# Filler work beside attention heads: smaller weight splits asked for earlier, less of it ahead of the heads and more inside them, and waits per tile in the pools

## The chip, the cores and the metric

One core of one Trainium2 chip runs the kernel. The metric is the device time of one execution in microseconds (us). The engines are TensorE (PE, with its weight loads PEld), VectorE (DVE), ScalarE (ACT), GpSimd (POOL) and SyncE (SP), whose queue issues nearly all DMAs, in order.

## The reference

One block of a hybrid conformer, for 1024 tokens of width 1024, float32:

```
h = rms_norm(x); z = h @ w_in            # glu, q, k, v, gate logits
a = silu(rms_norm(causal_conv31(a_val * sigmoid(a_gate))))
y_a = a @ w_conv_out
o = three dilated window attentions, mixed by softmax of their lse   # 16 heads of 64
y_b = o @ w_attn_out
x = x + (g_a * y_a + g_b * y_b) @ w_out  # g = sigmoid(gate_logits + gate_b)
x = x + (silu(u_gate) * u_val) @ w_down  # u = causal_conv3(rms_norm(x) @ w_up)
```

The three windows of a head are computed as one masked attention: `mask[h]` holds, for each distance, what is added to a score.

## The kernel before

**Precision and its price.** Every product is made from two parts: `split` (L74) rounds a float32 tile to `hi` on ACT and takes `lo = src - hi` on DVE. A product is then three matmuls (hi*hi, hi*lo, lo*hi), and each weight piece of 128x1024 costs one DMA (`stage`, L79, recorded at L81, four `raw` buffers), one ACT and one DVE instruction (`wpiece`, L90). `gemm_half` (L103) makes a 128x512 result in 8 steps of three 128x512 matmuls (L108 to L110), and yields after each step, so that a caller can place steps one by one.

**Stages.** First come the norm, the transposes, the GLU and the q, k, v products, with the 31-tap convolution on DVE beside them (L366); q, k and v are spilled to DRAM. Then attention, then the merge with the output projections (L596 to L660), the up-projection (L670 to L800) and the down-projection (L806 on). Each stage has a tile pool of its own (`ph1`, `ph2` at L458, `hb2` at L596, `ph3` at L597, `ph4r`, `ph4`, `ph5`; `hb1` from the start).

**Filler.** Two products have no part in attention and are cut into steps: the gates (16 pieces of `w_ch`, two halves each, `gate_steps`, L146) and the convolution's output (8 pieces of `w_co`, in `side_work`, L459): 384 steps in all. A gate result goes to DRAM as `dgate`, a convolution output as `dya`. Some steps stand ahead of the heads: COVER = (24, 16, 52) are the steps taken before the convolution branch ends, between its two norm parts, and after the eight `da` spills (L428, L439, L454; the spills at L453). The rest is taken inside the heads by `fill`: FILL = (5.5, 9.5) sets how many steps a half head takes, 15 a head. What is left over runs behind the last head. The convolution's output needs `aT`, which `load_split` (L165) reads back from `da` and splits, 1024 columns at a time.

**Heads.** `head` (L486) loads q, kh, kl (two halves each), the mask m and v of one head by `fetch` (L132, recorded at L133), two buffers of each. `step` (L546) works on half a head: for each of four query tiles `score` (L501) makes q*kh and q*kl into PSUM (L507, L508), DVE adds the mask and reduces (L512), ACT takes the exponent in place (L514), DVE the reciprocal (L515) and POOL scales (L516). Beside it, `flip` (L519) transposes the scaled tiles of the half head before on PE (L523) and splits them (ph on ACT L76, pl on DVE L77), and `weigh` (L530) multiplies v by both (L531, L532). The output pair goes to DRAM (`do`, L578) after every second head. Between these, `fill` places filler steps:

```
rate = FILL[0] / 14 if prev is not None and prev[1] else FILL[1] / 10
```

**Merge.** `load_split` reads o back (`raw_o`), `merge` (L604) loads the two gates and y_a (`gg`, L608 to L610), multiplies o by the pieces of w_attn_out (`yb`, weights `raw_ao`, `hi_ao`, `lo_ao`) and forms the sum.

**What orders the work.** A scheduler with a model of the engines' times puts the instructions of each engine and each DMA queue into one fixed order when the kernel is built; the order of the program text is the priority. Pools decide waits: in a pool that reuses memory of an earlier pool, an instruction waits for what used that memory. Waits are attached to the instructions of the fixed orders.

Of the kernel before, what the change touches and what calls it, by code (L numbers as in the profile page):

```python
# [12 lines left out]
F32 = mybir.dt.float32  # L13
F32R = mybir.dt.float32r
AF = mybir.ActivationFunctionType
ALU = mybir.AluOpType
# [4 lines left out]
P = 128  # L21
D = 1024
T = 1024
# [8 lines left out]

LAG = 2
PEND = 2
FILL = (5.5, 9.5)
COVER = (24, 16, 52)


C_CW = 0
# [11 lines left out]
def block_kernel(ctx: ExitStack, tc: tile.TileContext, x, g1, g2, pack, mask,  # L51
# [13 lines left out]
    def bank_ps(name):  # L65
        return psB.tile([P, 512], F32, tag="B", name=name)
# [7 lines left out]
    def split(hi, lo, src):  # L74

        act.activation(hi, src, AF.Copy)  # L76
        dve.tensor_tensor(out=lo, in0=src, in1=hi.bitcast(F32), op=ALU.subtract)  # L77

    def stage(src, name):  # L79
        raw = wp.tile([P, 1024], F32, tag="raw", bufs=4, name=f"raw_{name}")  # L80
        sp.dma_start(raw.rearrange("p (a b) -> p a b", a=src.shape[1]) if len(src.shape) == 3 else raw, src)  # L81
        return raw
# [20 lines left out]
    def gemm_half(o, w, actT, half):  # L103

        hi, lo = w
        ah, al = actT[0][half], actT[1][half]
        for k in range(KT):
            pe.matmul(o, hi[:, k, :], ah[:, k, :], start=(k == 0), stop=False)  # L108
            pe.matmul(o, hi[:, k, :], al[:, k, :], start=False, stop=False)  # L109
            pe.matmul(o, lo[:, k, :], ah[:, k, :], start=False, stop=(k == KT - 1))  # L110
            yield
# [34 lines left out]
    def gate_steps(hT):  # L146
        def gate(c, w, half):
            gp = bank_ps(f"gate_{c}_{half}")
            yield from gemm_half(gp, w, hT, half)
            sg = cst.tile([P, 512], F32, tag="f2", bufs=2, name=f"gs_{c}_{half}")  # L150
            act.activation(sg, gp, AF.Identity, bias=pk[:, C_GB + c : C_GB + c + 1])
            sp.dma_start(dgate[c][:, half * 512 : half * 512 + 512], sg)

        for c in range(12):
            w = wpiece(w_ch[16 + c], f"gt{c}")
            for half in range(2):
                yield from gate(c, w, half)
        ws = [wpiece(w_ch[16 + c], f"gt{c}") for c in range(12, 16)]
        for half in range(2):
            for c in range(12, 16):  # L160
                yield from gate(c, ws[c - 12], half)
            if half == 0:
                yield "half"
# [11 lines left out]
    hb1_cm = tc.tile_pool(name="hb1", bufs=1, side="right")  # L175
    hb1 = hb1_cm.__enter__()

    def hb_tiles(pl, name):
        t = [[pl.tile([P, KT, 512], F32R, tag=f"hb{a}{h}", name=f"{name}{a}{h}") for a in range(2)]
             for h in range(2)]  # L180
        return [[t[h][a] for h in range(2)] for a in range(2)]


    with tc.tile_pool(name="ph1", bufs=1) as p1:
# [239 lines left out]
                    if t is not None:  # L424
                        qkv_tail(*t)
        assert all(t is None for t in tails)
        gates = gate_steps(hT)
        for _ in range(COVER[0]):  # L428
            next(gates)
        conv_acc = conv_branch()  # L430
# [24 lines left out]
            next(gates)  # L455


    with tc.tile_pool(name="ph2", bufs=1) as p2:  # L458
        def side_work():  # L459

            left = []
            for t in gates:
                if t == "half":
                    aT = hb_tiles(hb1, "aT")
                    left = list(range(0, KT, 2))
                    wait = 0
                elif left:
                    if wait == 0:
                        load_split(aT, da, 0, "a", [left.pop(0)])
                    wait = (wait + 1) % 7  # L470
                yield
            assert not left
            left = list(range(0, KT, 2))
            for c0 in (0, 4):
                ws = [wpiece(w_co[c], f"co{c}") for c in range(c0, c0 + 4)]
                for half in range(2):
                    for c in range(c0, c0 + 4):
                        if left:
                            load_split(aT, da, 1, "a", [left.pop(0)])
                        yp = bank_ps(f"ya_{c}_{half}")  # L480
                        yield from gemm_half(yp, ws[c - c0], aT, half)
                        ya = cst.tile([P, 512], F32, tag="f2", bufs=2, name=f"ya_{c}_{half}")
                        act.activation(ya, yp, AF.Copy)
                        sp.dma_start(dya[c][:, half * 512 : half * 512 + 512], ya)

        def head(h):  # L486
            hp, r, g8 = h // 2, (h % 2) * DH, h // 8
            q = p2.tile([P, T], F32R, tag="q", bufs=2, name=f"q_{h}")
            kh = p2.tile([P, T], F32R, tag="kh", bufs=2, name=f"kh_{h}")
            kl = p2.tile([P, T], F32R, tag="kl", bufs=2, name=f"kl_{h}")  # L490
            m = p2.tile([P, T], F32, tag="m", bufs=2, name=f"m_{h}")
            v = p2.tile([P, 8, P], F32R, tag="v", bufs=2, name=f"v_{h}")
            for s in range(2):
                fetch(q[s * DH : (s + 1) * DH, :], dq[g8][s][r : r + DH, hp % 4, :])
                fetch(kh[s * DH : (s + 1) * DH, :], dk[g8][0][r : r + DH, hp % 4, :])
                fetch(kl[s * DH : (s + 1) * DH, :], dk[g8][1][r : r + DH, hp % 4, :])
            sp.dma_start(m, mask[h])
            fetch(v, dv[h // 8][:, h % 8, :, :])
            return q, kh, kl, v, m

        def score(h, tiles, i):  # L501
            q, kh, kl, v, m = tiles
            nk = (i + 1) * P
            s = big_ps(f"s_{h}_{i}")
            for c0 in range(0, nk, 512):
                n = min(512, nk - c0)
                pe.matmul(s[:, c0 : c0 + n], q[:, i * P : (i + 1) * P], kh[:, c0 : c0 + n], start=True, stop=False)  # L507
                pe.matmul(s[:, c0 : c0 + n], q[:, i * P : (i + 1) * P], kl[:, c0 : c0 + n], start=False, stop=True)  # L508
# [3 lines left out]
            dve.tensor_tensor_reduce(out=pt, in0=s[:, :nk], in1=m[:, u0 : u0 + nk], scale=-1.0, scalar=3e38,  # L512
                                     op0=ALU.add, op1=ALU.min, accum_out=st[:, 0:1])
            act.activation(pt, pt, AF.Exp, bias=st[:, 0:1], scale=-1.0, accum_out=st[:, 1:2])  # L514
            dve.reciprocal(st[:, 2:3], st[:, 1:2])  # L515
            pool.tensor_scalar(pt, pt, st[:, 2:3], 1.0, op0=ALU.mult, op1=ALU.mult)  # L516
            return pt

        def flip(h, half, pts, kt):  # L519
            q0 = max(0, kt - half * 4)  # L520
            pp = bank_ps(f"pp_{h}_{half}_{kt}")
            for qb in range(q0, 4):
                pe.transpose(pp[:, qb * P : (qb + 1) * P], pts[qb][:, kt * P : (kt + 1) * P], ident)  # L523
# [3 lines left out]
            split(ph[:, c], pl[:, c], pp[:, c])  # L527
            return kt, ph, pl, c

        def weigh(o, v, nkt, kt, ph, pl, c):  # L530
            pe.matmul(o[:, c], v[:, kt, :], ph[:, c], start=(kt == 0), stop=False)  # L531
            pe.matmul(o[:, c], v[:, kt, :], pl[:, c], start=False, stop=(kt == nkt - 1))  # L532

        filler = side_work()

        credit = [0.0]

# [55 lines left out]
            pass  # L593


    hb2 = ctx.enter_context(tc.tile_pool(name="hb2", bufs=1))  # L596
    with tc.tile_pool(name="ph3", bufs=1) as p3:  # L597
        oT = hb_tiles(hb2, "oT")
        for half in range(2):
            load_split(oT, do_, half, "o")  # L600
# [105 lines left out]
        p4r_cm = tc.tile_pool(name="ph4r", bufs=1, side="right")  # L706
# [24 lines left out]
        transpose_raw(*tails.pop(0))  # L731
        assert not tails

    with tc.tile_pool(name="ph4", bufs=1) as p4:
# [68 lines left out]
    p4r_cm.__exit__(None, None, None)  # L803


    with tc.tile_pool(name="ph5", bufs=1) as p5_:  # L806
# [180 lines left out]
```

## Time and profile before

| | |
|---|---|
| time, median of 3 runs | 1809.56 us (1807.88 to 1813.9) |
| the profiled execution | 1811.24 us |
| its span on the core | 1809.5 us |
| mean granted PE clock | 0.992 |
| instructions | 22485 |
| PE busy, 575 to 950 us (heads) | 363.94 of 375 us |

A row of a group reads: line, engine, operation, output <- inputs, shape, count | busy us, mean ns of one | idle time of the engine just before, and what ended it. A row of a timeline: start in us, duration, engine, line, operation, and in brackets the wait ahead of it with what ended it. A row of a window: from and to, length, then busy us and (x number of instructions) of PE, PEld, DVE, ACT and POOL, the granted PE clock, the busy share of the DMA engines and GB/s. A row of waits: engine, instruction, what it waited for, total us, times, longest.

### The profile page before, as it was taken

The page shows a single profiled execution, that of the slowest core. Times are in us where ns is not written, and L with a number is a line of the kernel's source. Part 1 is how long each engine was busy: PE and PEld are TensorE (multiplying, and loading weights), DVE is VectorE, ACT ScalarE, POOL GpSimd, SP SyncE. Part 2 cuts the span into 40 slices and gives each one's busy share as a digit, 9 for nine tenths or more (in the row PEclk, how much of TensorE's full clock was granted, in tenths as well). Part 3 has the DMA queues.
Part 4 walks back from the last instruction along what each step waited for, and adds up shares of the span by engine and source line. Part 5 has one row for each costly group of instructions (what it writes and reads, how often), then busy time and mean ns, then how long its engine had stood idle before and what let it go on. Part 6 is the DMA issues. An engine that isn't in the chain of part 4 may idle for free.

```text
span 1809.5 us, 22485 instructions
## 1 busy us (share of the span) xinstructions
PE 1771.3 (98%) x8248; PEld 1464.5 (81%) x8248; DVE 1320.5 (73%) x1801; ACT 771.8 (43%) x1203; POOL 194.5 (11%) x197
## 2 busy tenths in 40 slices
PE   8999999999999999999999999989999999999999
PEld 6888888888877888878888878768888888878887
DVE  6999999999635656665645543787777777789863
ACT  5111132223245656665655332545444554543441
POOL 1000142132002212222210000210000000000000
PEclk9999999999999999999999999999999999999999
DMA  5111145345468546664527543312222122389851
GB/s 210 49 49 47 41 134 175 105 134 169 139 200 246 135 136 177 201 195 142 152 78 268 179 152 134 99 47 108 79 82 82 71 95 91 116 304 333 298 181 47
DMA packets 141920, 257.05 MB, mean 142 GB/s; under 512 B 11249, under 2 KB 60529, under 8 KB 141810
## 3 DMA queue, kind: packets, MB, share of 16 engines
q1 hardware_dynamic: 141808, 255.61, 43.6%
q8 instruction: 65, 1.06, 0.2%
q14 instruction: 45, 0.37, 0.1%
q10 hardware_dynamic: 2, 0.00, 0.0%
HBM read 189.51 MB, written 66.06 MB: 141 GB/s over the span
## 4 chain that ended last, share of the span: by engine, by line
PE 53%; DMA 4%; DVE 3%; issue 1%; ACT 1%; SPq 1%; POOLq 0%; POOL 0%; DVEq 0%; ACTq 0%
PE xz L673 5%; PE xz L674 5%; PE xz L675 5%; PE dx L832 5%; PE dy L832 5%; DMA gg<-dya 2%; PE pp L523 2%; PE y L673 2%; PE y L675 2%; PE y L674 2%; PE ya L108 2%; PE ya L109 2%; PE ya L110 2%; PE wo L126 2%; PE o L531 2%; PE wo L125 2%
## 5 line engine op out<-in xcount | busy, mean ns | idle before, releaser
L366 DVE SCALAR_TENSOR_TENSOR cacc<-apad,pk,cacc 128x1024 f32<-128x1024 f32 x240 | 298.1, 1278 | 0.7
L125 PE MATMUL qkv<-hi_qkv,hT 128*128 128x512 f32 x384 | 151.9, 397 | 0.0
L127 PE MATMUL qkv<-hi_qkv,hT 128*128 128x512 f32 x384 | 150.5, 392 | 0.0
L126 PE MATMUL qkv<-lo_qkv,hT 128*128 128x512 f32 x384 | 149.5, 390 | 0.0
L512 DVE CUSTOM_DVE_ANT_0 p<-s,m 128x128 f32<-128x128 f32 (+7 forms) x128 | 95.2, 751 | 67.3 <-PE pp L523 43.4
L77 DVE TENSOR_TENSOR pl<-pp,ph 128x512 fp32r<-128x512 f32 x192 | 102.9, 550 | 48.9 <-ACT ph L76 48.4
L76 ACT ACTIVATE ph<-pp 128x512 fp32r<-128x512 f32 x192 | 90.9, 487 | 96.4 <-PE pp L523 92.3
L516 POOL TENSOR_SCALAR p<-p,st 128x128 f32<-128x128 f32 (+7 forms) x128 | 94.8, 749 | 339.8 <-DVE st L515 219.5
L772 DVE SCALAR_TENSOR_TENSOR u<-u,pk 128x1023 f32<-128x1023 f32 (+1 forms) x88 | 112.4, 1280 | 18.8 <-ACT u L770 18.5
L101 POOL TENSOR_TENSOR rs<-ss,mhalf 128x8 f32<-128x8 f32 x32 | 73.8, 2311 | 338.0 <-DVE ss L100 338.0
L514 ACT ACTIVATE p<-p,st 128x128 f32<-128x128 f32 (+7 forms) x128 | 99.0, 775 | 15.8 <-DVE st L512 14.0
L108 PE MATMUL gate<-hT,hi_gt 128*128 128x512 f32 x256 | 102.6, 401 | 0.0
L109 PE MATMUL gate<-hT,hi_gt 128*128 128x512 f32 x256 | 101.5, 396 | 0.0
L110 PE MATMUL gate<-hT,lo_gt 128*128 128x512 f32 x256 | 100.8, 395 | 0.0
L523 PE MATMUL pp<-ident,p 128*128 128x128 f32 x576 | 94.0, 276 | 0.0
L127 PEld LDWEIGHTS qkv<-hi_qkv,hT 128*128 128x128 f32 x384 | 72.1, 188 | 15.5
L126 PEld LDWEIGHTS qkv<-lo_qkv,hT 128*128 128x128 f32 x384 | 72.2, 188 | 14.4
L125 PEld LDWEIGHTS qkv<-hi_qkv,hT 128*128 128x128 f32 x384 | 72.2, 188 | 14.0
L507 PE MATMUL s<-kh,q 128*128 128x512 f32 (+1 forms) x192 | 69.6, 367 | 9.5 <-DVE st L512 6.2
L523 PEld LDWEIGHTS pp<-ident,p 128*128 128x128 f32 x576 | 69.2, 142 | 10.0 <-issue 0.2
L531 PE MATMUL o<-ph,v 128*128 128x512 f32 x192 | 72.9, 380 | 3.8 <-ACT ph L76 1.6
L532 PE MATMUL o<-pl,v 128*128 128x512 f32 x192 | 70.4, 368 | 1.8 <-DVE pl L77 1.8
(289 smaller groups left out, 4612.8 us busy)
## 6 DMA issues: line engine op xcount, KB each, us to landing
wr<-w_down SPq DMA_DIRECT2D x45, 512.0 KB, 5.8
gr<-dff SPq DMA_DIRECT2D x62, 256.0 KB, 5.4
raw_qkv<-w_qkv SPq DMA_DIRECT2D x24, 512.0 KB, 4.1
raw_uv<-w_up SPq DMA_DIRECT2D x22, 512.0 KB, 3.2
raw_ug<-w_up SPq DMA_DIRECT2D x22, 512.0 KB, 3.2
dff<-u SPq DMA_DIRECT2D x22, 512.0 KB, 2.6
dv<-v SPq DMA_DIRECT2D x16, 512.0 KB, 3.2
raw_gt<-w_ch SPq DMA_DIRECT2D x16, 512.0 KB, 4.6
```

Source lines behind the costliest of these rows:

```text
L108: pe.matmul(o, hi[:, k, :], ah[:, k, :], start=(k == 0), stop=False)
L109: pe.matmul(o, hi[:, k, :], al[:, k, :], start=False, stop=False)
L110: pe.matmul(o, lo[:, k, :], ah[:, k, :], start=False, stop=(k == KT - 1))
L125: pe.matmul(ps, ah, hi[:, k % 2, :], start=(k == 0), stop=False)
L126: pe.matmul(ps, ah, lo[:, k % 2, :], start=False, stop=False)
L127: pe.matmul(ps, al, hi[:, k % 2, :], start=False, stop=(k == KT - 1))
L366: dve.scalar_tensor_tensor(out=acc, in0=a[:, j : j + T], scalar=w(j), in1=acc, op0=ALU.mult, op1=ALU.add)
L523: pe.transpose(pp[:, qb * P : (qb + 1) * P], pts[qb][:, kt * P : (kt + 1) * P], ident)
L673: pe.matmul(o, wh[:, k, :], bh[:, k, :], start=(start and k == 0), stop=False, skip_group_check=not start)
L674: pe.matmul(o, wh[:, k, :], bl[:, k, :], start=False, stop=False, skip_group_check=not start)
L675: pe.matmul(o, wl[:, k, :], bh[:, k, :], start=False, stop=(k == 3), skip_group_check=not start)
L832: pe.matmul(banks[n], a[:, c], b[:, d], start=(start and i == 0 and m == 0), stop=(stop and i == nf - 1 and m == 2), skip_group_check=True)
```

## The change

- **Halves.** `wpiece2` splits a filler weight in two halves of 512 columns each, and `load_split` does the same for `aT` and o.
- **Pieces ahead.** `ahead` takes a list of uses (weight, name, consumer) and asks for weight pieces up to two ahead of the one in use, at most four in hand.
- **One filler.** Gates and convolution output are joined into one generator, `side_steps`, made before the convolution ends. The loads of `aT` are spread, one with each half-1 gate of the last four pieces and then one with each convolution output.
- **How much, where.** COVER is (24, 16, 20) instead of (24, 16, 52), FILL (6.5, 11.5) instead of (5.5, 9.5): 18 steps a head.
- **Order.** The score's reduce and exponent, and the split of a flipped block, are issued with `high_priority(URGENT)`, 120.
- **Pools.** `hb1`, `ph2`, `hb2`, `ph3`, `ph4r`, `ph4` and `ph5` are made with `reuse_waits="tile"`, so that a tile waits for the earlier tiles whose memory it takes and not for the whole pool's; q, kh, kl, v and the first four p tiles go to a pool of their own, `ph2in`.

Line numbers are some 20 higher behind the new functions.

```diff
-FILL = (5.5, 9.5)
-COVER = (24, 16, 52)
+FILL = (6.5, 11.5)
+COVER = (24, 16, 20)
+URGENT = 120
...
+    HALVES = (slice(0, 512), slice(512, 1024))
+    def wpiece2(src, name):
+        raw = stage(src, name)
+        hi = wp.tile([P, 1024], F32R, tag="whi", bufs=4, name=f"hi_{name}")
+        lo = wp.tile([P, 1024], F32R, tag="wlo", bufs=4, name=f"lo_{name}")
+        for c in HALVES:
+            split(hi[:, c], lo[:, c], raw[:, c])
+        return [t.rearrange("p (a b) -> p a b", a=KT) for t in (hi, lo)]
+    def ahead(uses, more=2):
+        keys = list(dict.fromkeys(n for _, n, _ in uses))
+        src = {n: w for w, n, _ in uses}
+        last = {n: i for i, (_, n, _) in enumerate(uses)}
+        got = {}
+        for i, (_, n, consumer) in enumerate(uses):
+            while len(got) < min(len(keys), keys.index(n) + 1 + more):
+                k = len(got)
+                if k >= 4 and last[keys[k - 4]] >= i:
+                    break
+                got[keys[k]] = wpiece2(src[keys[k]], keys[k])
+            yield from consumer(got[n])
+    def side_steps(hT, da):
+        aT = []
+        left = [(h, k) for h in range(2) for k in range(0, KT, 2)]
+        def gate(c, half):
+            def go(w):
+                gp = bank_ps(f"gate_{c}_{half}")
+                if c >= 12 and half == 1:
+                    if not aT:
+                        aT.extend(hb_tiles(hb1, "aT"))
+                    load_split(aT, da, 0, "a", [left.pop(0)[1]])
+                yield from gemm_half(gp, w, hT, half)
...
+        return ahead([gate(c, half) for c in range(12) for half in range(2)]
+                     + [gate(c, half) for half in range(2) for c in range(12, 16)]
+                     + [conv_out(c, half) for c0 in (0, 4) for half in range(2) for c in range(c0, c0 + 4)])
...
             raw = stage(src[:, k : k + 2, half * 512 : half * 512 + 512], f"{name}{half}{k}")
-            split(dst[0][half][:, k : k + 2, :], dst[1][half][:, k : k + 2, :],
-                  raw.rearrange("p (a b) -> p a b", a=2))
+            for i, c in enumerate(HALVES):
+                split(dst[0][half][:, k + i, :], dst[1][half][:, k + i, :], raw[:, c])
...
-        gates = gate_steps(hT)
+        gates = side_steps(hT, da)
...
-    with tc.tile_pool(name="ph2", bufs=1) as p2:
+    with tc.tile_pool(name="ph2", bufs=1, reuse_waits="tile") as p2, \
+            tc.tile_pool(name="ph2in", bufs=1, reuse_waits="tile") as p2i:
...
-            q = p2.tile([P, T], F32R, tag="q", bufs=2, name=f"q_{h}")
+            q = p2i.tile([P, T], F32R, tag="q", bufs=2, name=f"q_{h}")
...
-            pt = p2.tile([P, nk], F32, tag=f"p{i}", bufs=1, name=f"p_{h}_{i}")
+            pt = (p2i if i < 4 else p2).tile([P, nk], F32, tag=f"p{i}", bufs=1, name=f"p_{h}_{i}")
...
+            with tc.high_priority(URGENT):
+                dve.tensor_tensor_reduce(out=pt, in0=s[:, :nk], in1=m[:, u0 : u0 + nk], scale=-1.0, scalar=3e38,
+                                         op0=ALU.add, op1=ALU.min, accum_out=st[:, 0:1])
+                act.activation(pt, pt, AF.Exp, bias=st[:, 0:1], scale=-1.0, accum_out=st[:, 1:2])
...
+            with tc.high_priority(URGENT):
+                split(ph[:, c], pl[:, c], pp[:, c])
...
-        filler = side_work()
+        filler = gates
...
-    hb2 = ctx.enter_context(tc.tile_pool(name="hb2", bufs=1))
-    with tc.tile_pool(name="ph3", bufs=1) as p3:
+    hb2 = ctx.enter_context(tc.tile_pool(name="hb2", bufs=1, reuse_waits="tile"))
+    with tc.tile_pool(name="ph3", bufs=1, reuse_waits="tile") as p3:
```

The same argument is added to `hb1`, `ph4r`, `ph4` and `ph5`.

More of the change, by code (lines that the diff above doesn't have):

```diff
@@ L144, in block_kernel @@
     dx2 = [dr.tile([P, D], F32, name=f"dx2_{i}") for i in range(8)]
[L146 to L163, printed above, removed]
+    HALVES = (slice(0, 512), slice(512, 1024))
@@ L168, in load_split @@
             raw = stage(src[:, k : k + 2, half * 512 : half * 512 + 512], f"{name}{half}{k}")
-            split(dst[0][half][:, k : k + 2, :], dst[1][half][:, k : k + 2, :],
-                  raw.rearrange("p (a b) -> p a b", a=2))
+            for i, c in enumerate(HALVES):
+                split(dst[0][half][:, k + i, :], dst[1][half][:, k + i, :], raw[:, c])
     edge = ctx.enter_context(tc.tile_pool(name="edge", bufs=1, side="right"))
     edge.tile([P, 248], F32, name="edge")
-    hb1_cm = tc.tile_pool(name="hb1", bufs=1, side="right")
+    hb1_cm = tc.tile_pool(name="hb1", bufs=1, side="right", reuse_waits="tile")
     hb1 = hb1_cm.__enter__()
@@ L455, in block_kernel @@
             next(gates)
-    with tc.tile_pool(name="ph2", bufs=1) as p2:
[L459 to L484, printed above, removed]
+    with tc.tile_pool(name="ph2", bufs=1, reuse_waits="tile") as p2, \
+            tc.tile_pool(name="ph2in", bufs=1, reuse_waits="tile") as p2i:
         def head(h):
             hp, r, g8 = h // 2, (h % 2) * DH, h // 8
-            q = p2.tile([P, T], F32R, tag="q", bufs=2, name=f"q_{h}")
-            kh = p2.tile([P, T], F32R, tag="kh", bufs=2, name=f"kh_{h}")
-            kl = p2.tile([P, T], F32R, tag="kl", bufs=2, name=f"kl_{h}")
+            q = p2i.tile([P, T], F32R, tag="q", bufs=2, name=f"q_{h}")
+            kh = p2i.tile([P, T], F32R, tag="kh", bufs=2, name=f"kh_{h}")
+            kl = p2i.tile([P, T], F32R, tag="kl", bufs=2, name=f"kl_{h}")
             m = p2.tile([P, T], F32, tag="m", bufs=2, name=f"m_{h}")
-            v = p2.tile([P, 8, P], F32R, tag="v", bufs=2, name=f"v_{h}")
+            v = p2i.tile([P, 8, P], F32R, tag="v", bufs=2, name=f"v_{h}")
             for s in range(2):
@@ L705, in block_kernel @@
         hb1_cm.__exit__(None, None, None)
-        p4r_cm = tc.tile_pool(name="ph4r", bufs=1, side="right")
+        p4r_cm = tc.tile_pool(name="ph4r", bufs=1, side="right", reuse_waits="tile")
         p4r = p4r_cm.__enter__()
@@ L732, in block_kernel @@
         assert not tails
-    with tc.tile_pool(name="ph4", bufs=1) as p4:
+    with tc.tile_pool(name="ph4", bufs=1, reuse_waits="tile") as p4:
         for n in ("b22", "t4"):
@@ L803, in block_kernel @@
     p4r_cm.__exit__(None, None, None)
-    with tc.tile_pool(name="ph5", bufs=1) as p5_:
+    with tc.tile_pool(name="ph5", bufs=1, reuse_waits="tile") as p5_:
         keep3 = {}
```

18 lines of the change are left out of this document (14 added, 4 removed).

## The prediction, made before the changed kernel was run

> **What bounds the kernel now.** I read the page's engine totals first, then the table of 50-us windows, then TensorE's waits for the stretch that the change touches.
>
> ```profile
> PE 1771.3 (98%) x8248; PEld 1464.5 (81%) x8248; DVE 1320.5 (73%) x1801; ACT 771.8 (43%) x1203; POOL 194.5 (11%) x197
> 100.00:150.00 50.00, 50.00 (x222) 41.39 (x222) 47.95 (x41) 7.13 (x7) 0.00 (x0) 1.00 0.15 50
> 500.00:550.00 50.00, 45.01 (x198) 36.37 (x197) 18.80 (x31) 22.27 (x30) 0.67 (x2) 0.96 0.67 211
> 1150.00:1200.00 50.00, 40.70 (x174) 31.33 (x173) 46.34 (x45) 26.10 (x36) 14.03 (x6) 0.93 0.22 74
> 575.00:950.00 375.00, 363.94 (x1960) 305.87 (x1959) 227.84 (x582) 229.90 (x496) 86.77 (x116) 0.99 0.53 154
> ```
>
> A window row gives its length, then busy time and instructions of PE, PEld, DVE, ACT and POOL, then the granted clock. TensorE (PE) is busy 98% of the span, and a full window holds 222 matmuls in 50 us: one 128x512 matmul every 0.225 us. The changed order issues the same matmuls, so their sum cannot move; only the holes can. PE's 38.2 idle us (1809.5 - 1771.3) lie in a few places: 5.0 in 500 to 550, where the heads begin, 11.06 in 575 to 950, the heads (375 - 363.94), 9.3 in 1150 to 1200, the rest at both ends and in single waits. A hole also costs clock: the heads run at 0.99, which is up to 3.6 us more (1% of 363.94). So the heads can give about 15 us at most, and the question is which holes close and which open.
>
> ```profile
> PE s L507 <- DVE st L512: 6.2, 9, 1.3
> PE s L507 <- DMA kl<-dk: 3.0, 1, 3.0
> PE o L532 <- DVE pl L77: 1.8, 1, 1.8
> PE o L531 <- ACT ph L76: 1.6, 2, 1.1
> PE o L531 <- DVE op L575: 1.5, 5, 0.6
> PE y L674 <- DVE blk_t L77: 4.7, 1, 4.7
> PE y L673 <- ACT hi_s L76: 2.6, 1, 2.6
> ```
>
> These are PE's waits by kind (total us, times, longest), the first five from 500 to 960. In the heads, scores wait for the reduce of VectorE (DVE) two scores back, and weighings for the split of the flipped block. The one long wait is head 0's first load.
>
> **Part 1: COVER 52 to 20, the start of attention.** Thirty-two steps of three matmuls leave the cover ahead of the heads; in the changed kernel's order of PE, 72 of those 96 matmuls stand behind the first score instead of ahead of it, 72 x 0.225 = 16.2 us. They are work that still has to be done, so the start gains or loses by one comparison: how much earlier the first score can begin against 16.2 us of work not yet done.
>
> ```profile
> 540.59 0.39 PE L110 MATMUL gate<-hT,lo_gt 128*128 128x512 f32 x1
> 543.97 0.47 PE L507 MATMUL s<-kh,q 128*128 128x128 f32 x2 [3.00 <-DMA kl<-dk]
> 545.05 0.47 PE L508 MATMUL s<-kl,q 128*128 128x128 f32 x2 [0.61 <-DMA kl<-dk]
> 526.45 1.06 SPq L152 DMA_DIRECT2D dgate<-gs  x1
> 532.79 0.51 SPq L133 DMA_DIRECT2D q<-dq  x1
> 536.44 0.60 SPq L133 DMA_DIRECT2D kl<-dk  x1
> L453 SPq DMA_DIRECT2D da<-cacc x8: 319/320/1012, 517.0 to 525.9; - x8
> DMA to landing us min/median/max: 2.6/3.3/6.8
> DMA to landing us min/median/max: 3.9/5.5/7.1
> DMA to landing us min/median/max: 6.4/7.5/8.5
> SPq L133 <- DMA da<-cacc: 5.1, 2, 3.9
> ```
>
> The three landing rows are those of da, q and kl. Today the last cover matmul is issued at 540.59, the first score at 543.97. SyncE's queue (SP) issues DMAs in order. Up to the gate spill issued at 526.45 (dgate of piece 4, first half) the two kernels' queues agree: eight da spills, a weight load, this spill. In before, the loads of head 0 then wait for da to land and for a second gate spill, so that q goes at 532.79 and the second kl at 536.44. In after the eight loads stand directly behind the 526.45 spill, each with a wait for its own tile. So they can issue from about 527.5, which the edit is right about: 5.3 us earlier.
>
> But the landing gains less. The last da spill, issued at 525.9, lands 6.8 us later at 532.7; with the gate spill behind it that is about 533.3. In before the loads land some 1.3 us apart: the second q at 535.2 + 7.1 = 542.3, the second kl two loads later at 536.44 + 8.5 = 544.9. If the six loads queue behind the spills at that pace, the fifth, the second kh, which the first score needs, lands at 533.3 + 5 x 1.25 = 539.5. The other end is loads that do not queue at all: the second kl issued at 527.5 + 3.65 = 531.2 (same spacing as 532.79 to 536.44), landing the shortest q time later, 3.9, at 535.1. The late end is no gain at all, 543.97. Cost = first score's move + 16.2: 539.5 - 543.97 + 16.2 = **+11.7** (+7.3 to +16.2). I take 11.7, since the queue was full in just these microseconds (kl's landings of 6.4 to 8.5 against q's first 3.9). PE, whose cover would end at 540.8 - 16.2 = 524.6, would stand idle about 15 us in one piece. Nothing fills that hole: PE's order is fixed, and behind the cover come only scores and flips until the first softmax is through, because the next filler's PSUM bank comes after those of the flips.
>
> [...]
>
> ```profile
> 551.17 0.41 PE L523 MATMUL pp<-ident,p 128*128 128x128 f32 x1
> 544.00:552.00 8.00, 6.32 (x19) 4.75 (x20) 4.64 (x16) 4.50 (x11) 2.08 (x4) 0.63 1.05 275
> ```
>
> From the second kl to the first flip 6.1 us pass (545.05 to 551.17), with 16 score matmuls in them; in after only the 8 of the first four scores stand there, so some 8 x 0.225 = 1.8 us more are uncovered: **+2** (0 to +5, the whole chain less the score matmuls). The granted clock is 0.63 over these 8 us, 3.0 us lost, after a hole of 3.0; it will be lost again after the longer hole, so it is no difference. [...]
>
> **Part 2: the heads (FILL, halves, URGENT, two pieces ahead).** Each head carries 18 filler steps instead of 15: 16 x 9 = 144 matmuls more, which are the 96 of the cover and 48 of the stretch behind the last head.
>
> ```profile
> L77 DVE TENSOR_TENSOR lo_gt<-raw_gt,hi_gt 128x1024 fp32r<-128x1024 f32 x16 | 20.1, 1256 | 16.5 <-ACT hi_gt L76 16.5
> L77 DVE TENSOR_TENSOR pl<-pp,ph 128x512 fp32r<-128x512 f32 x96 | 64.9, 686 | 28.3 <-ACT ph L76 27.9
> L76 ACT ACTIVATE hi_gt<-raw_gt 128x1024 fp32r<-128x1024 f32 x16 | 16.9, 1056 | 24.8 <-PE gate L109 23.5 <-PE qkv L127 1.3
> L76 ACT ACTIVATE ph<-pp 128x512 fp32r<-128x512 f32 x96 | 56.1, 595 | 53.9 <-PE pp L523 51.9 <-PE o L532 0.6
> 809.87 3.49 DVE L77 TENSOR_TENSOR aT<-raw_a,aT 128x1024 fp32r<-128x1024 f32 x3
> 800.00:850.00 50.00, 46.74 (x235) 38.80 (x236) 30.24 (x76) 30.16 (x64) 12.74 (x17) 0.93 0.63 186
> ```
>
> A weight split is 1.26 us of DVE in one piece today; in halves it would be 2 x 0.69 = 1.37 (priced by the 128x512 row), on ACT 2 x 0.60 = 1.19 against 1.06. For some 40 pieces that is 5 us on each, hidden by 147 idle us of DVE in the heads (375 - 227.84) unless it falls ahead of a reduce. The holes come from such splits: three aT splits make one block of 3.49 us, and that window loses most, 3.3 us idle at a clock of 0.93. Halving helps if something urgent comes between the halves. In the changed order it mostly doesn't: 26 of 32 filler pieces of the heads have both halves side by side on DVE, 17 of 25 such blocks stand directly ahead of a score's reduce (before: 9 of 18), and one block of three to four pieces (4.8 us by these durations) is left. What does help: 18 steps instead of 15 put about 1.4 us more PE work between a score and its flip (16.6 to 18.0 us, counted in PE's order), and 0.2 more between flip and weighing, which covers most waits of 1.3 us at most. Of the 15 us I take a third, **-6**; the ends are -15 (all holes close) and +5 (seven more blocks at 0.69 each). URGENT's edit has the same answer: it is seen only in the order, which these counts use.
>
> **Part 3: the stretch behind the last head.**
>
> ```profile
> 947.73 0.32 SPq L578 DMA_DIRECT2D do<-op  x1
> 962.04 2.00 SPq L81 DMA_DIRECT2D raw_ao<-w_ao  x2
> 974.60 0.39 PE L108 MATMUL yb<-oT,hi_ao 128*128 128x512 f32 x1
> L77 DVE TENSOR_TENSOR lo_ao<-raw_ao,hi_ao x4: 1224/1226/1226, 969.6 to 975.7; 128x1024 fp32r<-128x1024 f32 x4
> DMA to landing us min/median/max: 3.9/5.2/7.0
> ```
>
> Behind the last weighing stood 125 matmuls of conv_out up to the first yb; in after 77 are left, 48 x 0.225 = 10.8 us less. What they hide is a chain: last do spill at 947.73, reload of o, the first w_ao piece at 962.04, 5.2 us of landing, its hi, its lo from 969.6, so ready at 970.8, while yb begins at 974.60: 3.8 us to spare. If the chain keeps its length, 10.8 - 3.8 = 7.0 us open up. It can be shorter, as fewer gate and dya transfers stand ahead of w_ao in SP's queue; but a dya spill is still ahead of it, ready only about 5.4 us before yb by PE's order, and a raw buffer must be free. So 4 to 6 us of hole plus up to 2 of clock: **+6** (0 if w_ao moves up by the whole 7; +11 if the spill that is ready 5.4 us before yb heads the full 8.8 us from w_ao's issue to its lo, and the clock falls).
>
> **Part 4: waits per tile in the later pools.** The last 2687 matmuls of PE stand in the same order. The largest hole there, 9.3 us in 1150 to 1200, has DVE at 46.34 of 50 us and waits for blk_t and hi_s, which no pool releases: **0** (-4 to +1).
>
> **Sum.** 11.7 + 2 - 6 + 6 = +13.7. The profiled execution took 1811.24 (span 1809.5 and 1.74 around it), 1.68 above the median of 1809.56. On the median: 1809.56 + 13.7 = 1823.
>
> **Rivals.** A measurement of this kernel can tell about 0.3% from no change, 5.4 us: faster is under 1804.1, slower over 1815.0.
>
> *Faster.* The DVE blocks stop being ahead of anything that PE needs soon: with 1.4 us more work between score and flip, and the longest score wait 1.3 us, all holes of the heads close: -15. Loads land at the early end (+7.3), the last chain shrinks by 7 (0): 1809.56 - 7.7 = 1802. For it: waits that short are easily covered. Against it: it needs three ends at once, and the da spills are in the queue. It decides when start and last stretch together cost under 9.6 us: 1 in 10.
>
> *The same.* The start costs 11.7 and 2, the first w_ao load moves up fully (0), and the heads give 12: +1.7, 1811. For it: SP's queue is less loaded behind the last head. 0.14.
>
> *Slower still.* The doubled number of split blocks directly ahead of a reduce decides in the heads (+5), with 11.7 + 2 at the start and 8 behind the heads: +26.7, 1836. For it: 17 such blocks against 9, one of 4.8 us. Against it: URGENT moves reduces ahead of what is not yet begun, and DVE has 39% idle. 0.07.
>
> *That the change doesn't do what it says*: halves side by side are whole splits, so the halving alone gives nothing; it is in the forecast already, as the -6 comes from the steps.
>
> **How the numbers follow.** The forecast has 0.69 and its own range 1815 to 1832; of it 0.02 fall within 0.3%, if the first loads come early. So faster 0.10, same 0.14 + 0.02 = 0.16, slower 0.67 + 0.07 = 0.74. The range leaves out the faster case and the end of the worst: 1806 to 1834, which takes in the unknown ends of landing (7.3 to 16.2) and of the last chain (0 to 11).
>
> **What would show it.** The wait of the first score for kl should be near 15 us, with PE's last gate matmul ahead of it near 525 and the first score at 539 to 540; a first score near 535 is the early end. The heads' idle time should go from 11 us to 5 to 8, with fewer waits for st. The first yb should wait for lo_ao or hi_ao for 4 to 6 us, and the window 1150 to 1200 should keep its 9.3 idle us, shifted. It would be wrong if PE had other work in the first hole, if the waits for st grew, or if the yb wait were absent.

## The result and the profile after

The changed kernel takes 1823.81 us (median of 4 runs, 1821.63 to 1824.43), the kernel before 1809.0 in the same comparison: ratio 1.0076, interval 1.0061 to 1.0092. That is 14.8 us slower; 1823 was predicted. The profiled execution took 1823.43 us, with a span of 1821.7, 12.2 more than that of before.

Page and 50-us windows of the changed kernel, with the 375 us of the heads as one row (columns as before); the last row is the kernel before in the window of the row above it:

```profile
PE 1768.1 (97%) x8248; PEld 1461.6 (80%) x8248; DVE 1324.9 (73%) x1841; ACT 776.4 (43%) x1243; POOL 197.9 (11%) x197
500.00:550.00 50.00, 32.09 (x142) 25.81 (x141) 21.41 (x42) 22.56 (x36) 3.84 (x6) 0.83 0.75 229
575.00:950.00 375.00, 367.00 (x1969) 307.73 (x1968) 223.03 (x584) 228.52 (x506) 87.42 (x113) 1.00 0.53 154
950.00:1000.00 50.00, 46.61 (x216) 38.12 (x215) 27.11 (x40) 27.87 (x46) 0.00 (x0) 0.97 0.73 247
950.00:1000.00 50.00, 50.00 (x223) 41.40 (x222) 25.81 (x30) 25.45 (x34) 0.00 (x0) 1.00 0.73 258
```

The same 8248 matmuls; the loss is in holes. The window of the start is idle for 17.9 us instead of 5.0, at a clock of 0.83. The heads are idle for 8.0 instead of 11.1. Behind them is a new hole, 3.4 us in 950 to 1000. PE's waits in the changed kernel (480 to 990, then two rows of 960 to 1260, and the one wait of `wo` in the kernel before):

```profile
PE s L521 <- DMA kh<-dk: 15.9, 2, 14.9
PE s L521 <- DVE st L527: 5.0, 9, 1.3
PE yb L109 <- ACT hi_ao L77: 3.0, 1, 3.0
...
PE o L547 <- ACT ph L77: 1.3, 3, 0.8
PE o L548 <- DVE pl L78: 0.9, 2, 0.7
PE o L547 <- DVE op L591: 0.6, 2, 0.3
...
PE yb L111 <- DVE lo_ao L78: 0.4, 1, 0.4
```

```profile
PE wo L126 <- ACT hi_wo L77: 2.0, 1, 2.0
PE wo L127 <- DVE lo_wo L78: 1.8, 1, 1.8
```

```profile
PE wo L126 <- DVE lo_wo L77: 2.1, 1, 2.1
```

One wait holds nearly all of the start's hole: the first score stands 14.9 us for kh of head 0. PE and SP around it:

```profile
523.22 0.39 PE L111 MATMUL gate<-hT,lo_gt 128*128 128x512 f32 x1
538.54 0.77 PE L521 MATMUL s<-kh,q 128*128 128x128 f32 x2 [14.93 <-DMA kh<-dk]
```

```profile
525.46 1.08 SPq L187 DMA_DIRECT2D dgate<-gs  x1
526.63 1.34 SPq L134 DMA_DIRECT2D q<-dq  x1
530.27 0.59 SPq L134 DMA_DIRECT2D kh<-dk  x1
```

The edit does what it says: q goes out at 526.63 instead of 532.79. But the second kh, issued at 530.27, lands 8.0 us later, and the first score begins only 5.4 us earlier (538.54 against 543.97), while 72 matmuls, 16.3 us at 0.2267 (the distance of two starts in the cover), no longer stand ahead of it.

To see where time goes without counting moved work as loss, I cut the span at starts of matmuls (the first score, the last filler matmul, the first `wo`, the first behind the last `wo`), and add 16.3 us to the first score's start where 72 matmuls moved behind it (0.2267 for each of the 24 in the run with COVER 36). Differences from the span of before, in us, each from one profiled execution:

| kernel | first score | first score to end of filler | wait of first yb, and merge | wo stage | rest | sum |
|---|---|---|---|---|---|---|
| after | +10.9 | -4.3 | +5.3 | +1.8 | -1.5 | +12.2 |
| e1, amounts of before | -3.1 | +0.2 | 0 | +3.0 | 0 | +0.1 |
| e2, amounts alone | +13.4 | -3.9 | +9.7 | +1.8 | -1.6 | +19.4 |
| e6, COVER 36 | +1.7 | -4.8 | 0 | +2.0 | -1.1 | -2.2 |
| e7, late pools as before | +12.1 | -3.6 | +8.4 | +0.7 | -1.4 | +16.2 |
| e11, COVER 44 | -2.6 | -8.4 | 0 | -2.0 | +0.9 | -12.0 |
| e12, and merge loop | -2.6 | -7.2 | 0 | -4.0 | +0.4 | -13.4 |

Terms are rounded, so a row can miss its sum by 0.1. Executions of one kernel differ by up to 10 us (1803.53 to 1813.51 in the ten of e6, 1806.57 to 1814.42 in the ten of e1), so a term of one profile can be off by some us, and verdicts go by the ratios.

### The profile page after: what moved, and what is told of

It is laid out like the page before. It is cut to its first block, busy times and chain, and to the rows that moved or that the text cites. A ratio compares the mean times of both kernels' runs of the same rounds, so it can differ in the third digit from the quotient of the medians.

```text
span 1821.7 us, 22591 instructions
## 1 busy us (share of the span) xinstructions
PE 1768.1 (97%) x8248; PEld 1461.6 (80%) x8248; DVE 1324.9 (73%) x1841; ACT 776.4 (43%) x1243; POOL 197.9 (11%) x197
## 4 chain that ended last, share of the span: by engine, by line
PE 87%; DMA 4%; DVE 4%; issue 2%; ACT 1%; SPq 1%; POOLq 0%; POOL 0%; DVEq 0%; ACTq 0%
PE dx L848 6%; PE xz L689 5%; PE xz L690 5%; PE xz L691 5%; PE dy L848 5%; PE qkv L128 5%; PE qkv L126 5%; PE qkv L127 5%; PE gate L109 3%; PE pp L538 3%; PE gate L110 3%; PE gate L111 3%; DMA gg<-dya 2%; PE y L689 2%; PE y L691 2%; PE y L690 2%
```

## The experiments

The theory at this point: the time is lost because work was taken out from ahead of the first score and from behind the last head (the amounts), and the other edits cost nothing. The rival: the other edits (halves, order, pools) cost it. The first four runs shared the runs of before (median 1808.63).

**e1_amounts_back**

```diff
-FILL = (6.5, 11.5)
-COVER = (24, 16, 20)
+FILL = (5.5, 9.5)
+COVER = (24, 16, 52)
```

> All edits stay, but COVER and FILL are those of before (24, 16, 52 and 5.5, 9.5). Theory (the 72 matmuls that left the cover cost the time, the other edits cost nothing): the cover ends near 540.8 again, head 0's loads go out from 527 and land by 541 to 542, so the start loses its hole of 15 us and also the 3.0 us wait of before; the stretch behind the heads has its 125 matmuls and no yb wait; the heads keep about 11 us idle. Time 1801 to 1808, that is 1 to 8 us under before. Rival (halves, order and pools cost the time): 1819 to 1825, with the lost time in the heads.

Measured: 1812.42, ratio 1.0015 (1.0003 to 1.0028). The 11 us that separate it from the changed kernel are the amounts, so the rival falls. But the gain that I expected did not come: the kernel is a little slower than before. Waits at the start, and later from 1000 on, in this kernel:

```profile
PE s L522 <- DMA kl<-dk: 0.6, 1, 0.6
...
PE wo L126 <- ACT hi_wo L77: 2.0, 1, 2.0
PE wo L127 <- DVE lo_wo L78: 1.7, 1, 1.7
```

The start's wait of 3.0 us is gone, as expected. The heads stay as they were, and the wo stage takes 3.0 us more: a new wait for hi_wo beside that for lo_wo makes 1.6 of them (3.7 us of waits instead of 2.1), and the rest is not in the waits. That wait became a question of its own (e8, e10).

**e2_amounts_alone**: the kernel before with `COVER = (24, 16, 20)`, `FILL = (6.5, 11.5)`.

> The kernel before with nothing changed but COVER (24, 16, 20) and FILL (6.5, 11.5). Theory: the start loses more than in the changed kernel, since the loads still wait for all of da to land: first score at 541 to 544 with the cover ending near 524.5, a hole of 17 to 19 us; the heads gain about 7 us from 18 steps a head instead of 15; the first yb waits 3 to 5 us. Time 1822 to 1830. Rival (the other edits cost the time): within 3 us of before, 1806 to 1812.

Measured: 1830.51, ratio 1.0119 (1.0104 to 1.0134), 0.5 above the range. Its waits from 480 to 575 and from 575 to 1000, and its heads:

```profile
PE s L507 <- DMA kl<-dk: 16.9, 1, 16.9
...
PE yb L108 <- ACT hi_ao L76: 6.8, 1, 6.8
PE s L507 <- DVE st L512: 3.6, 5, 1.2
```

```profile
575.00:950.00 375.00, 366.45 (x1963) 307.44 (x1961) 221.40 (x563) 227.44 (x482) 85.26 (x113) 1.00 0.53 154
```

So the amounts alone cost 22 us, and the other edits give 7 of them back: 2.5 at the start (hole 17.3 against 15.3 us) and about 4 at the first yb. The heads' gain (8.6 us idle instead of 11.1) comes with the 18 steps, without halves and without priority.

**e3_no_urgent**: both `with tc.high_priority(URGENT):` taken away.

> The changed kernel without the high priority of the score's reduce and exponent and of the flip's split. Theory: the heads' gain comes from 18 steps a head, so this costs 0 to 3 us: 1822 to 1827. Rival (the priority made the heads' gain of 7 us): 1829 to 1832, idle time of TensorE between 575 and 950 back at 11 us or more.

Measured: 1825.27, ratio 1.0089 (1.0074 to 1.0104); the changed kernel's interval ends at 1.0092, so no difference is shown. The waits of the heads' scores (575 to 950) give the same row in both kernels:

```profile
PE s L521 <- DVE st L527: 4.4, 8, 1.3
```

**e4_whole_splits**: `HALVES = (slice(0, 1024),)`, and `load_split` as before.

> The changed kernel with filler weights, aT and o split in whole pieces of 1024 columns again. Theory: halves that stand side by side on DVE are whole splits, so the heads stay as they are and the time is within 3 us of the changed kernel, 1821 to 1827; a few tenths of a us of DVE per piece come back. Rival (the halves made the heads' gain): 1828 to 1832, with waits for the reduce as in before.

Measured: 1827.62 (1824.99 to 1833.48), ratio 1.0108 (1.0087 to 1.013). The time falls between the two ranges, just under the rival's. The medians differ by 3.8 us and the interval overlaps that of the changed kernel, so what the halves are worth is not settled by this run. Its profiled execution was the slowest of the four, so that its row (waits for st of 6.6 us) is no measure.

The next four (before: 1808.51) ask what sets the start and the stretch behind the heads.

**e5_spill_other_queue**

```diff
-            sp.dma_start(da[:, c, :], ct)
+            act.dma_start(da[:, c, :], ct)
```

> The changed kernel with the eight da spills issued from ScalarE's DMA queue instead of SyncE's; nothing else moves, head 0's loads still go out behind the gate spill at about 525.5. Theory (the loads queue behind the spills in one row of DMA rings): without them in the same row the loads land 3 to 4 us earlier, first score at 534 to 536 instead of 538.3, time 1819 to 1821. Rival (the sixteen DMA engines are shared, whoever issues, and their bandwidth is the limit): first score at 537.5 to 540, time 1822 to 1826.

Measured: 1821.81, ratio 1.0076 (1.0055 to 1.0098). Wait, spills and loads in this kernel (the landing row is that of kh):

```profile
PE s L521 <- DMA kh<-dk: 16.3, 2, 15.0
```

```profile
L493 ACTq DMA_DIRECT2D da<-cacc x8: 326/326/750, 516.4 to 525.3; - x8
```

```profile
DMA to landing us min/median/max: 8.0/8.0/8.0
```

The spills left SP's queue and the loads land no sooner. The time lies between the two ranges; the first score, at 539.0 us instead of 538.5, lies in the rival's. So that loads and spills stand in one queue is not what decides here; neither the rings that the theory names nor the shared engines and the limit of the rival are shown by it. It does not follow that the loads don't wait for the spills: by the views below they come behind them in both kernels, with slow slices from 531 where the spills are in SP's queue and from 531.75 here.

**e9_spill_early** (one execution, run with the last set) takes the spills away altogether:

```diff
+        for tt in range(8):
+            sp.dma_start(da[:, tt, :], xt[tt])
...
-            sp.dma_start(da[:, c, :], ct)
```

> The changed kernel with the eight da spills gone from the start of the heads: the convolution's result is left out, and eight spills of x, of the same size, are made near the start of the kernel instead, so that aT holds other data. Head 0's loads then stand ahead of the gate spill. What is read is their landing alone. Theory (the 4 MB of spills still under way hold the loads up): landing 3.9 to 6 us after issue, the second kh 4 to 6 us after the first load's issue plus its own place in the row. Rival (six loads of 256 KB are slow by themselves): landings of 7 to 8 us after issue as in the changed kernel, without any spill before them. The time may fall to 1812 to 1820 in either case, as the loads also go out earlier.

Measured: 1817.4. The view of DMA from 510 to 540 in 40 slices of 0.75 us, of this kernel, of the changed one, of e5 and of before (first row: busy tenths of the 16 DMA engines; second row: GB/s):

```profile
DMA  2898200620000000006989899999999999999999
GB/s 93 306 240 317 93 0 0 246 104 0 0 0 0 0 0 0 0 0 246 257 213 388 257 208 218 224 202 240 235 202 218 213 268 432 426 377 175 229 202 213
```

```profile
DMA  9850017009999998999998899999999999999999
GB/s 213 289 224 0 0 71 279 0 0 399 421 404 421 415 421 317 410 388 421 426 197 191 224 421 410 426 401 423 218 235 213 219 218 235 229 208 213 224 317 421
```

```profile
DMA  9871007203999999799969999999999999999999
GB/s 320 235 317 71 0 0 276 74 0 158 421 421 399 421 415 426 306 426 352 210 213 289 410 426 421 412 410 388 363 224 208 224 197 246 224 208 218 186 213 344
```

```profile
DMA  5379300800599999989999979999700096987998
GB/s 216 134 197 377 126 0 0 322 27 0 235 415 426 399 426 415 426 355 396 429 388 238 254 235 393 426 426 396 298 25 14 0 137 235 290 257 191 191 208 229
```

Here no spill of da is under way, and nothing else either up to 523.5 (zeros); then a gate spill of 256 KB (issued at 522.96) and a weight load of 512 KB (523.45) go ahead of the loads. Still they land like this:

```profile
L134 SPq DMA_DIRECT2D kh<-dk x3: 451/587/587, 524.4 to 530.3; - x3
...
DMA to landing us min/median/max: 5.9/7.6/10.0
```

The first two are head 0's, 5.9 and 7.6 us, the third is head 1's. From the issue of the first load (523.87) to the first score (534.01) 10.1 us pass; in the changed kernel 11.9 (526.63 to 538.54). The views divide these times. In this kernel ten slices of 202 to 257 GB/s begin at 526.5, in the changed one ten of 208 to 235 at 531: 1.66 MB in each, about the 1.57 MB of the six loads. So, as an estimate from bytes and the order of issue, the loads themselves take 7.5 us in both. Before that 2.6 us pass here, with the gate spill and the weight load, and 4.4 us in the changed kernel, with the spills. Some 1.2 us of either would pass with an empty queue too: in before nothing is under way when the first load goes out at 532.79 (0 GB/s from 533.25), and bytes flow from 534 on. So the transfers ahead cost about 1.4 us here and 3.2 in the changed kernel; the two costs are estimates, their difference of 1.8 is measured. In e5 the ten slow slices begin at 531.75, also behind the spills, though these are in another queue. So both theory and rival hold in part: the loads are slow by themselves, and the transfers ahead of them add some 3 us. While the loads run, DMA engines that are 8 to 9 tenths busy move about half of what they move while the da spills run (202 to 257 GB/s against 388 to 426 in most of the spills' slices). Head 0's six loads are each on one half of the partitions, the spills on all 128. That partitions set the rate is not shown by it: by bytes and order, the weight load of 512 KB on 128 partitions lies in the three slices from 525 of the changed kernel, and these have 191 to 224 too. Of the 4.5 us by which the first score comes earlier here (534.01), 1.8 are the shorter wait and 2.7 the earlier issue.

**e6_cover_36**: `COVER = (24, 16, 36)`, `FILL = (6.0, 10.6)`.

> The changed kernel with COVER (24, 16, 36) and FILL (6.0, 10.6): 48 matmuls more than in the changed kernel stand ahead of the first score (24 fewer than before) and 102 instead of 77 behind the last head. Theory (the hole at the start is the landing of head 0's loads less the cover): cover to 534, first score still at 538 to 539, so the hole falls from 15 to about 4.5 us and the first yb waits 0 to 1; with some 1.5 us of the heads' gain given back 1809 to 1815. Rival (the loads are late because of the other edits and slip along with the cover): 1818 or more.

Measured: 1807.97, ratio 1.0001 (0.9986 to 1.0016), better than expected. PE around the first score:

```profile
535.64 0.39 PE L111 MATMUL gate<-hT,lo_gt 128*128 128x512 f32 x1
540.24 0.77 PE L521 MATMUL s<-kh,q 128*128 128x128 f32 x2 [4.21 <-DMA kh<-dk]
```

Forty-eight matmuls put back ahead of the score (10.9 us) move the cover's end by 12.4 us and the score by 1.7: the loads do not move with the cover. The hole is the landing less the cover, and with 102 matmuls behind the last head the first yb does not wait.

**e7_late_pools**: `reuse_waits="tile"` taken from hb2, ph3, ph4r, ph4 and ph5.

> The changed kernel with waits for the whole pool again in hb2, ph3, ph4r, ph4 and ph5. Theory (the later pools' tile waits change nothing that TensorE waits for): within 2.5 us of the changed kernel, 1821 to 1826. Rival (they gave back part of the loss behind the heads): 1827 to 1832, with a longer first yb wait or longer waits from 1070 on.

Measured: 1827.05, ratio 1.0108 (1.009 to 1.0127). The orders are those of the changed kernel; the first yb waits longer:

```profile
PE yb L109 <- ACT hi_ao L77: 5.8, 1, 5.8
```

Against 3.0 that is 2.8 us, and the time is 3.2 us longer. The intervals just touch, so that the times alone show no difference; but wait and time agree, and the other kernels with these amounts and these pools wait 2.9 to 3.4 us there (e3, e4, e5, e9). So the rival holds: the tile waits of these five pools gain about 3 us, and they do it where the first yb waits.

**e8_sum_in_psum**, on e1:

```diff
-            dve.tensor_tensor(out=ya, in0=ya, in1=gb, op=ALU.add)
-            split(mT[0][half][:, c, :], mT[1][half][:, c, :], ya)
+            dve.tensor_tensor(out=yp, in0=ya, in1=gb, op=ALU.add)
+            split(mT[0][half][:, c, :], mT[1][half][:, c, :], yp)
```

> All edits with the amounts of before (as in the first run of these experiments), and the merge's sum written into the PSUM tile of yb and split from there, so that a gg buffer is free one ACT and one DVE instruction earlier. Theory (the merge is a loop of a gg load, its sigmoids and the split behind them on ScalarE, about 6.4 us a merge against TensorE's 5.4, and its lag is what wo waits for at its start): gg loads come 5.5 to 5.9 us apart, the waits for hi_wo and lo_wo of 3.7 us together fall to 0 to 2, time 1808 to 1811. Rival (wo waits for its own weight loads): waits and time as without it, 1811 to 1814.

Measured: 1811.79, ratio 1.0029 (1.0015 to 1.0043): no gain, and gg loads still 6.47 us apart (mean of twelve; 6.15 in before, 6.41 in the changed kernel, 6.37 in e1). The trace shows why: the loop moved. DVE, then SP, in this kernel (gg has three buffers):

```profile
1036.74 0.69 DVE L629 TENSOR_TENSOR gg<-gg 128x512 f32<-128x512 f32 x1 [2.74 <-DMA gg<-dya]
1037.35 0.69 DVE L634 TENSOR_TENSOR yb<-gg 128x512 f32<-128x512 f32 x1
```

```profile
1032.07 0.32 SPq L624 DMA_DIRECT2D gg<-dgate  x1
1038.07 0.32 SPq L624 DMA_DIRECT2D gg<-dgate  x1
```

SP's waits from 985 to 1057:

```profile
SPq L624 <- DVE yb L634: 58.4, 12, 6.2
```

In DVE's order the product of the tile being loaded (L629) stands ahead of the sum (L634) that frees the next buffer. So a load waits for a sum, which waits behind a product, which waits for a load: 6.0 us a turn here.

The last three (before: 1806.96) look for a better version and settle the loop.

**e10_merge_loop**: e6, the sum in PSUM, and

```diff
-            dve.tensor_tensor(out=ya, in0=ya, in1=ga, op=ALU.mult)
+            pool.tensor_tensor(out=ya, in0=ya, in1=ga, op=ALU.mult)
```

> COVER 36 and FILL (6.0, 10.6) as in the sixth run, with the merge's sum in PSUM and the product of y_a with its gate on GpSimd, so that neither ScalarE's nor VectorE's order ties a gg load to the sum of the next merge. Theory (the loop of the merge lags behind TensorE and wo pays for it): gg loads at most 5.7 us apart, waits for hi_wo and lo_wo from 3.9 down to 0 to 1.5, time 1804 to 1806.5. Rival (wo waits for its own weight loads): the waits stay, 1807 to 1809.

Measured: 1804.95, ratio 0.9988 (0.9977 to 0.9999), against 1.0001 (0.9986 to 1.0016) without it in the set before. SP's loads of three merges:

```profile
1027.40 0.32 SPq L624 DMA_DIRECT2D gg<-dgate  x1
1032.84 0.32 SPq L624 DMA_DIRECT2D gg<-dgate  x1
1038.28 0.32 SPq L624 DMA_DIRECT2D gg<-dgate  x1
```

The turns are 5.44 us (so is the mean of twelve; 6.40 in e6), PE's own pace (24 x 0.2267), and both waits of wo are gone from its list; the wo stage takes 91.5 us instead of 97.5. So the loop and its hold on wo are shown. What it is worth in time is not: 4 us of those 6 reach the end of the span in the two profiles, the ratios differ by 2.4 us, and their intervals overlap.

**e11_cover_44**: `COVER = (24, 16, 44)`, `FILL = (5.8, 10.2)`.

> The changed kernel with COVER (24, 16, 44) and FILL (5.8, 10.2): the first score has the 2194 matmuls of before ahead of it, each head carries 16 steps, 101 matmuls stand behind the last head. Theory (cover and the stretch behind the heads set the loss, the heads' gain comes with each further step): no hole at the start, first yb waits 0 to 1, heads 1 to 4 us better than with 15 steps; 1803 to 1808. Rival (the heads' gain needs 17 to 18 steps a head): 1809 to 1813, as with 15 steps.

Measured: 1798.42, ratio 0.9952 (0.9936 to 0.9969), far better than expected. **e12_cover_44_loop** adds the edits of e10.

> COVER 44 and FILL (5.8, 10.2) together with the merge's sum in PSUM and its product on GpSimd. Theory: the gains add, 2 to 3.5 us under the kernel with COVER 44 alone: 1800 to 1805. Rival: wo waits for its own weights, no difference to that kernel.

Measured: 1794.01, ratio 0.9933 (0.9917 to 0.995), below the range, the fastest version, 13 us under before; the intervals of the two overlap, so what the loop adds here, 4.4 us by the medians, is likely and not shown. Heads of e11, then of e1, then waits of e12 from 1000 to 1260 (no wait of wo stands in the list):

```profile
575.00:950.00 375.00, 367.27 (x2000) 310.33 (x1999) 228.11 (x599) 240.44 (x523) 84.05 (x112) 1.00 0.56 161
```

```profile
575.00:950.00 375.00, 362.53 (x1951) 302.73 (x1950) 228.05 (x596) 233.37 (x516) 87.31 (x115) 1.00 0.56 158
```

```profile
PE y L690 <- DVE blk_t L78: 4.7, 1, 4.7
PE tq L654 <- issue: 0.8, 1, 0.8
```

The two heads rows differ by one step a head, 16 against 15, and by 4.7 us idle. In e11 no score of the heads waits for st; in e1 twelve do, for 5.0 us; with 18 steps eight, for 4.4, and with the 16.6 of e6 four, for 1.6. So the gain does not grow with the steps. A filler piece is 16 steps (two halves of 8), so that with 16 steps a head each head uses up one piece: in DVE's order the splits of heads 2 to 7 then all stand behind the same score, and in e1 they drift from the second to the eighth. That this is the reason is argued, not shown.

## Why the prediction was right, and where it wasn't

- **Start, +11.7 and +2 (7.3 to 16.2).** Measured +10.9 for the first score, 538.54 against a forecast of 539.5, and a hole of 15 us. The comparison, how much earlier the loads land against the work taken away, is the mechanism: e6 and e11 close the hole by cover alone. That the loads queue behind the spills is borne out too: by the views it costs some 3 us, where 4.4 lie between the forecast's 539.5 and its early end of 535.1. With nothing ahead of them they would land near 535.3 (526.63 + 1.2 + 7.5, an estimate from the views of e9), but no run shows it. The parts of the sum were less good than the sum. The transfers ahead were through at 531 and not at 533.3, and the second kh landed 7.3 us behind that (530.27 + 8.0 = 538.3) and not 5 x 1.25 = 6.25. Nor is one queue for both the reason (e5), and the landings of before that grew from 3.9 to 8.5 us were no sign of spills: the last da spill had landed at 532.7, before the first of those loads was issued (532.79). The +2 between first score and first flip did not come: the first flip stands 4.1 us behind the first score (542.60) and not 7.2. In its place the first scores of head 1 wait another 2.5 us for their own loads (0.92 at 548.67, 1.56 at 550.53), which the prediction did not have. Both lie in the second column.
- **Heads, -6 (with the +2, -4).** Measured -4.3 for the whole column. e2 shows that the amounts bring it. The reason given, that 18 steps cover the waits for st, is not borne out: they are nine as before, the longest still 1.3 us, and their sum went from 6.2 to 5.0. The waits of the weighings (ph, pl, op) fell more, from 4.9 to 2.8. With 16 steps no score waits (e11). So the size of this term was luck. The count that I used for the risk, split blocks directly ahead of a reduce, tells nothing: e11 has 14 such blocks of 21, and no score waits.
- **Behind the last head, +6 (0 to 11).** Measured +5.3: 3.2 of hole, where 4 to 6 were forecast, and 2.1 in the merge behind it, where a second wait (0.4) and a lower clock (0.97) are. The up to 2 us of clock in the forecast were a term that no run shows; in its place the changed kernel shows a granted clock of 0.60 from 984 to 988 and of 0.97 from 988 to 992, behind the hole of 3.0, by estimate 1.7 us lost (4 x 0.40 + 4 x 0.03). The chain is the right one, but it is shorter than I made it. Last do spill, first w_ao load and hi_ao in the changed kernel, then hi_ao before:

```profile
965.23 0.32 SPq L594 DMA_DIRECT2D do<-op  x1
978.81 1.80 SPq L82 DMA_DIRECT2D raw_ao<-w_ao  x2
L77 ACT ACTIVATE hi_ao<-raw_ao x4: 1057/1057/1063, 983.3 to 988.5; 128x1024 fp32r<-128x1024 f32 x4
```

```profile
L76 ACT ACTIVATE hi_ao<-raw_ao x4: 1059/1061/1063, 968.5 to 974.6; 128x1024 fp32r<-128x1024 f32 x4
```

  The first yb needs hi_ao alone, which was ready at 969.6 before; I had ended the chain at lo_ao, 970.8. So 5.0 us were to spare and not 3.8. From the do spill to hi_ao 19.1 us pass instead of 21.8: w_ao goes out 13.6 us behind the spill instead of 14.3, and its hi begins 4.5 us later instead of 6.5. So 10.9 - 5.0 - 2.7 = 3.2 (48 matmuls at 0.2267).
- **Later pools, 0 (-4 to +1).** As a sum right (+1.8 and -1.5), as a statement wrong: the tile waits of these pools are worth 3 us at the first yb (e7). What I had missed is that hb2 and ph3 serve the stretch of part 3.
- **Sum.** 12.2 by the profiled spans, 14.8 by the medians, 13.7 forecast.

Of the rivals, "faster" needed the early landing and all holes of the heads closed; neither came; its sum of 1802 also leaves out the +2. That the halves do nothing by themselves is left open by e4.

## What to carry to other kernels

Work taken from in front of a wait must be weighed against how much earlier the awaited thing can land, not against how much earlier it is issued: here 6.2 us earlier in issue were 5.4 in the first score, and 16 us of work were gone. Filler should be given out in amounts that just cover both ends (here 84 steps ahead of the first score and some 100 matmuls behind the last head), and what is left then goes inside. Where buffers are reloaded in a loop, look in each engine's order for an instruction on the tile just being loaded that stands ahead of the one that frees the next buffer: moving it to an idle engine, with the sum kept in PSUM, took a loop of 6.4 us to PE's 5.44.

## What the runs showed of the hardware that was not expected

In the views of e9 and of the changed kernel, six loads of 256 KB on 64 partitions each move 202 to 257 GB/s with the DMA engines 8 to 9 tenths busy, and in the changed kernel the da spills, 512 KB on 128 partitions, 388 to 426 in most of their slices in the same state. So the busy share of the DMA engines did not tell here how much they moved: head 0's loads fill the engines at half the rate, with the spills ahead of them or without (e9). The mask and v, 512 KB on 128 partitions each and also loads, come behind them in a stretch of 377 to 432 GB/s (the slices from 534.75 to 537 of the view of e9), so it is not that they are loads. The cause is open all the same: the weight load ahead of them, also on 128 partitions, has slices of 191 to 224. A version of the kernel that loads q, kh and kl on all 128 partitions at once was not tried.

By the views, the loads of one queue wait behind spills that another engine's queue issued (e5): their slow slices begin at 531.75, against 531 with both in one queue.
